# A decoder layer on one core: weight buffers 4160 and 4128 bytes apart instead of 4096

## The chip, the cores and the metric

The kernel runs on one NeuronCore of a Trainium2 chip. The metric is device time in microseconds. The kernel before takes 413.82 us, the median of three runs (413.51, 413.82, 414.05). Work is spread over TensorE (PE; its weight loads are listed as PEld), VectorE (DVE), ScalarE (ACT), GpSimd (POOL) and SyncE (SP, which issues the loads of weights). SBUF is the on-chip memory of 128 partitions; a tile takes the same range of bytes in each partition, and that range's start is called its place here.

## The reference

One hybrid decoder layer in float32 on 256 tokens with D = 1024. Two token mixers (an RWKV-7 recurrence and causal attention over one block of 256) read one combined projection; their outputs are gated, merged and projected; a gated MLP with a width-3 causal convolution follows.

```
h = rms_norm(x, norm1_g);  proj = h @ w_in              # 1024 x 5408
y_a = rwkv7_time_mix(shifted part of proj)              # 8 heads of 64
y_b = moba_attention(q, k, v)                           # 8 heads of 64
x = x + (sigmoid(g_a) * (y_a @ w_branch_a) + sigmoid(g_b) * (y_b @ w_branch_b)) @ w_out
h2 = rms_norm(x, norm2_g);  u = h2 @ w_ffn_up           # 1024 x 5632
x = x + (gelu(causal_conv3(u[:, :2816])) * u[:, 2816:]) @ w_ffn_down
```

## The kernel before

Every big product is split for precision. A weight tile of 128 x 1024 float32 (4 KB in a partition) is loaded into a `raw` buffer. ScalarE rounds it to TensorE's shorter format into a `whi` buffer (line 238, in a few early cases VectorE), and VectorE writes the remainder raw - whi into a `wlo` buffer (line 248). Activations are split in the same way (`hh` and `hl` are the two halves of `hx`; `mh`/`ml`, `yah`/`yal`, `ybh`/`ybl` and `hb` are others). A product is then the sum of three: high x high, high weight x low activation, low weight x high activation.

Four `raw`, four `whi` and three `wlo` buffers rotate (line 51). `weights` hands out a ready pair and makes the next; `load_next` issues the next load on SP. Each matmul has one operand that is loaded into the array (128 columns) and one that is streamed past it (256 or 512 columns). Which is which differs:

- `wst` (lines 278, 280, 283): weights loaded, 256 columns of activations streamed. Most projections and both branch products.
- `xst` (lines 299, 300, 303): activations loaded, 512 columns of weights streamed. The attention's projections (with `hx`) and the output projection (with `mh`, `ml`).
- `up` (lines 1160, 1163), the FFN's first product: weights loaded, `hx` streamed, 512 columns for the high weights (both halves of the activations at once) and 256 for the low ones.
- `down` (lines 1178, 1180, 1182), its second: `hb` loaded, 512 columns of weights streamed.

The pools of tiles lie one behind the other in a partition: `cst` (constants, `hx`, and the four buffers that hold `yah`, `yal`, `ybh`, `ybl` among others), then `wp` (`raw`, `whi`, `wlo`), then `sb` (everything else: x, `hb`, `mh`, `ml`, the work tiles). Places in bytes, as the program is built:

| tile | before | modulo 512 |
|---|---|---|
| hx (cst) | 29760 | 64 |
| ybh, ybl, yah, yal (cst) | 46144, 50240, 54336, 58432 | 64 |
| raw, four | 71040 and every 4096 | 384 |
| whi, four | 87424 and every 4096 | 384 |
| wlo, three | 103808 and every 4096 | 384 |
| first tile of sb | 116096 | 384 |
| hb, eight places | 124288 to 161152 | 384 |
| ml, mh | 165248, 189824 | 384 |

Of the kernel before, what the change touches and what calls it, by code (L numbers as in the profile page):

```python
# [9 lines left out]
F32 = mybir.dt.float32  # L10
F32R = mybir.dt.float32r
# [25 lines left out]
def body(tc, x, positions, norm1_g, w_in, rwkv_mu, w_decay_up, decay_bias, w_aaa_up,  # L37
# [5 lines left out]
    with ctx:  # L43
        cst = ctx.enter_context(tc.tile_pool(name="cst", bufs=1))
        wp = ctx.enter_context(tc.tile_pool(name="wp", bufs=1))
        sb = ctx.enter_context(tc.tile_pool(name="sb", bufs=1))
        ps = ctx.enter_context(tc.tile_pool(name="ps", bufs=1, space=PSUM))
        dr = ctx.enter_context(tc.tile_pool(name="dr", bufs=1, space=DRAM))

        joined = [False]  # L50
        NB4, NRAW, NHI, NLO = 10, 4, 4, 3

# [166 lines left out]
        def load_next(first=False, into=None):  # L219
            if queue:  # L220
                ap = queue.pop(0)
                k, c = ap.shape[1], ap.shape[2]
                raw = wp.tile([128, 1024], F32, name="raw", tag="raw", bufs=NRAW) if into is None else into
                rv = raw[:, :k * c].rearrange("p (k c) -> p k c", k=k)
                for ks in ((slice(0, 2), slice(2, 4)) if first else (slice(0, k),)):
                    nc.sync.dma_start(rv[:, ks], ap[:, ks])
                raws.append((raw, k, c))
# [3 lines left out]
        def split_hi():  # L231
            if raws:
                nhi[0] += 1
                eng = dve if nhi[0] in (4, 5, 6) else act
                raw, k, c = raws.pop(0)
                hi = wp.tile([128, 1024], F32R, name="whi", tag="whi", bufs=NHI)
                if eng is act:
                    act.copy(hi[:, :k * c], raw[:, :k * c])  # L238
                else:
                    eng.tensor_copy(hi[:, :k * c], raw[:, :k * c])  # L240
                halves.append((raw, hi, k, c))

        def split_lo(eng=dve):
            if halves:
                raw, hi, k, c = halves.pop(0)
                n = k * c
                lo = wp.tile([128, 1024], F32R, name="wlo", tag="wlo", bufs=NLO)
                eng.tensor_tensor(lo[:, :n], raw[:, :n], hi[:, :n].bitcast(F32), op=OP.subtract)  # L248
                ready.append((hi[:, :n].rearrange("p (k c) -> p k c", k=k),
                              lo[:, :n].rearrange("p (k c) -> p k c", k=k)))  # L250
                nlo[0] += 1
                if not NRAW < nlo[0] <= NRAW + 4:
                    load_next()

        def weights(n=1):

            w = ready.pop(0)
            for _ in range(n):
                split_lo()
                split_hi()  # L260
            return w
# [76 lines left out]
        def first_steps():  # L338
# [58 lines left out]
                                         hh[:, k].bitcast(F32), op0=OP.mult, op1=OP.subtract)  # L397

            def tiles(nm):
                return wp.tile([128, 1024], F32R, name=nm, tag=nm, bufs=NHI if nm == "whi" else NLO)  # L400


            raw, _, _ = raws.pop(0)
            hi, lo = tiles("whi"), tiles("wlo")
            hs = [slice(i * 512, i * 512 + 512) for i in range(2)]
            dve.tensor_copy(hi[:, hs[0]], raw[:, hs[0]])
# [7 lines left out]
            for k in range(4):  # L414
                low(k)
            split_hi()
            high(6)
            high(7)
            for k in range(4, 8):
                low(k)  # L420
            split_lo()
            split_hi()
            split_lo()
            split_hi()
            p = acc()
# [846 lines left out]
```

## Time and profile before

| | before |
|---|---|
| median of the timed runs, us | 413.82 |
| the profiled execution, us | its span, 411.9; the page has no other time of it |
| HBM read, written | 68.76 MB, 1.44 MB, 170 GB/s over the span |
| TensorE busy from 210 to 306 us (the FFN) | 96.00 of 96.00 us |
| VectorE busy in that stretch | 76.52 us |
| ScalarE busy in that stretch | 55.42 us |
| costliest lines of the chain | acc L1160 15%, acc L1163 7%, L278, L280 and L283 7% each |

A row of the groups reads: line, engine, operation, output<-inputs, shapes, xcount, then the busy time in us and the mean duration of one in ns, then the idle time of the engine just ahead and what ended it. Matmul records overlap each other, since the engine is pipelined. A row with three durations gives the shortest, the median and the longest.

### The profile page before, as it was taken

The page shows a single profiled execution, that of the slowest core. Times are in us where ns is not written, and L with a number is a line of the kernel's source. Part 1 is how long each engine was busy: PE and PEld are TensorE (multiplying, and loading weights), DVE is VectorE, ACT ScalarE, POOL GpSimd, SP SyncE. Part 2 cuts the span into 40 slices and gives each one's busy share as a digit, 9 for nine tenths or more (in the row PEclk, how much of TensorE's full clock was granted, in tenths as well). Part 3 has the DMA queues.
Part 4 walks back from the last instruction along what each step waited for, and adds up shares of the span by engine and source line. Part 5 has one row for each costly group of instructions (what it writes and reads, how often), then busy time and mean ns, then how long its engine had stood idle before and what let it go on. Part 6 is the DMA issues. An engine that isn't in the chain of part 4 may idle for free.

```text
span 411.9 us, 8111 instructions
## 1 busy us (share of the span) xinstructions
PE 404.6 (98%) x3199; PEld 355.6 (86%) x3199; DVE 322.2 (78%) x559; ACT 230.8 (56%) x384; POOL 38.3 (9%) x62
## 2 busy tenths in 40 slices
PE   6999999999999999999999999999999999999996
PEld 3999989888899998999988888888888888888885
DVE  2888999869557876678974898979779678797784
ACT  5799645465444765453653884646446455464450
POOL 8910070000210010120000000000000000000000
PEclk9999999999999999999999999999999999999999
DMA  8955565663483352466564555765665666656612
GB/s 247 314 190 154 156 179 157 163 171 105 95 226 94 104 155 68 146 202 198 175 197 147 160 199 183 225 202 176 199 193 171 199 200 198 200 168 199 198 53 102
DMA packets 61765, 70.72 MB, mean 172 GB/s; under 512 B 8349, under 2 KB 52195, under 8 KB 61728
## 3 DMA queue, kind: packets, MB, share of 16 engines
q1 hardware_dynamic: 60768, 69.41, 56.3%
q0 software_dynamic: 944, 0.80, 0.9%
q8 instruction: 25, 0.41, 0.4%
q14 instruction: 12, 0.10, 0.1%
q10 hardware_dynamic: 16, 0.00, 0.0%
HBM read 68.76 MB, written 1.44 MB: 170 GB/s over the span
## 4 chain that ended last, share of the span: by engine, by line
PE 89%; DVE 4%; ACT 3%; DMA 1%; issue 1%; SPq 0%; POOL 0%; ACTq 0%
PE acc L1160 15%; PE acc L1163 7%; PE acc L278 7%; PE acc L283 7%; PE acc L280 7%; PE at L1160 5%; PE acc L299 5%; PE f L1182 4%; PE acc L303 4%; PE f L1180 4%; PE acc L300 4%; PE f L1178 4%; PE at L1163 2%; ACT sc L970 2%; DMA x<-in_x_dram 1%
## 5 line engine op out<-in xcount | busy, mean ns | idle before, releaser
L238 ACT CAST whi<-raw 128x1024 fp32r<-128x1024 f32 x120 | 125.8, 1051 | 113.6 <-PE acc L1160 26.2
L248 DVE TENSOR_TENSOR wlo<-raw,whi 128x1024 fp32r<-128x1024 f32 x120 | 145.7, 1218 | 41.8 <-PE acc L1163 12.9
L1160 PE MATMUL acc<-hx,whi 128*128 128x512 f32 x264 | 72.4, 395 | 0.0
L278 PE MATMUL acc<-hx,whi 128*128 128x256 f32 x232 | 58.2, 287 | 0.0
L280 PE MATMUL acc<-hx,whi 128*128 128x256 f32 x232 | 56.0, 278 | 0.0
L1160 PEld LDWEIGHTS acc<-hx,whi 128*128 128x128 f32 x264 | 45.3, 188 | 6.3
L1163 PEld LDWEIGHTS acc<-hx,wlo 128*128 128x128 f32 x264 | 40.2, 188 | 6.1
L278 PEld LDWEIGHTS acc<-hx,whi 128*128 128x128 f32 x232 | 43.6, 188 | 1.6 <-issue 0.7
L280 PEld LDWEIGHTS acc<-hx,whi 128*128 128x128 f32 x232 | 43.7, 188 | 0.1
L1163 PE MATMUL acc<-hx,wlo 128*128 128x256 f32 x264 | 41.3, 278 | 0.0
L283 PE MATMUL acc<-hx,wlo 128*128 128x256 f32 x232 | 35.9, 277 | 0.0
L1182 PE MATMUL f<-wlo,hb 128*128 128x512 f32 x80 | 31.3, 391 | 0.0
L1180 PE MATMUL f<-whi,hb 128*128 128x512 f32 x80 | 31.2, 390 | 0.0
L1178 PE MATMUL f<-whi,hb 128*128 128x512 f32 x80 | 31.2, 390 | 0.0
L283 PEld LDWEIGHTS acc<-hx,wlo 128*128 128x128 f32 x232 | 30.7, 188 | 0.3 <-issue 0.3
L1160 PE MATMUL at<-hx,whi 128*128 128x512 f32 x88 | 24.0, 394 | 0.0
L1168 DVE TENSOR_REDUCE an<-acc 128x256 f32<-128x512 f32 x22 | 15.0, 689 | 6.5 <-PE acc L1163 5.6
L299 PE MATMUL acc<-whi,hx 128*128 128x512 f32 x48 | 19.3, 403 | 0.0
L300 PE MATMUL acc<-whi,hx 128*128 128x512 f32 x48 | 18.8, 391 | 0.0
L1182 PEld LDWEIGHTS f<-wlo,hb 128*128 128x128 f32 x80 | 15.0, 188 | 3.5 <-DVE wlo L248 0.4
L1178 PEld LDWEIGHTS f<-whi,hb 128*128 128x128 f32 x80 | 15.0, 188 | 2.8
L1180 PEld LDWEIGHTS f<-whi,hb 128*128 128x128 f32 x80 | 15.0, 188 | 2.8
(311 smaller groups left out, 700.4 us busy)
## 6 DMA issues: line engine op xcount, KB each, us to landing
raw<-in_w_ffn_up_dram SPq DMA_DIRECT2D x44, 512.0 KB, 4.3
raw<-in_w_in_dram SPq DMA_DIRECT2D x38, 512.0 KB, 4.5
raw<-in_w_ffn_down_dram SPq DMA_DIRECT2D x22, 512.0 KB, 3.3
raw<-in_w_out_dram SPq DMA_DIRECT2D x8, 512.0 KB, 4.3
x<-in_x_dram SPq DMA_DIRECT2D x8, 256.0 KB, 5.2
early<-in_w_in_dram SPq DMA_DIRECT2D x4, 512.0 KB, 9.8
raw<-in_w_branch_b_dram SPq DMA_DIRECT2D x4, 512.0 KB, 3.6
raw<-in_w_branch_a_dram SPq DMA_DIRECT2D x4, 512.0 KB, 4.1
```

Source lines behind the costliest of these rows:

```text
L238: act.copy(hi[:, :k * c], raw[:, :k * c])
L248: eng.tensor_tensor(lo[:, :n], raw[:, :n], hi[:, :n].bitcast(F32), op=OP.subtract)
L278: pe.matmul(om, wh[:, k, ms], xh[:, k0 + k], start=k0 + k + m == 0, stop=False, skip_group_check=True)
L280: pe.matmul(om, wh[:, k, ms], xl[:, k0 + k], start=False, stop=False, skip_group_check=True)
L283: pe.matmul(om, wl[:, k, ms], xh[:, k0 + k], start=False, stop=k0 + k == nk - 1 and m == n - 1, skip_group_check=True)
L299: pe.matmul(ps_[t], xh[:, K, ts], wh[:, k], start=K == 0, stop=False)
L300: pe.matmul(ps_[t], xl[:, K, ts], wh[:, k], start=False, stop=False)
L1160: pe.matmul(ps_[m], wh[:, k, ms], hx[:, k0 + k].rearrange("p a s -> p (a s)"), start=k0 + k == 0, stop=False, skip_group_check=True)
L1163: pe.matmul(ps_[m][:, 0:S], wl[:, k, ms], hh[:, k0 + k], start=False, stop=k0 + k == 7, skip_group_check=True)
L1178: pe.matmul(fin[f], hb[:, 0, i, ts], wh[:, 0, cs], start=st, stop=False, skip_group_check=f == 3)
L1180: pe.matmul(fin[f], hb[:, 1, i, ts], wh[:, 0, cs], start=False, stop=False, skip_group_check=f == 3)
L1182: pe.matmul(fin[f], hb[:, 0, i, ts], wl[:, 0, cs], start=False, stop=False, skip_group_check=f == 3)
```

## The change

The `whi` tiles are made 1040 elements wide in place of 1024 (4160 bytes), the `wlo` tiles 1032 (4128 bytes); the first 1024 of them are used, as before. At the start of `sb` a tile of 40 elements that nobody uses is added.

```diff
+        sb.tile([128, 40], F32, name="gap")
         joined = [False]
...
-                hi = wp.tile([128, 1024], F32R, name="whi", tag="whi", bufs=NHI)
+                hi = wp.tile([128, 1040], F32R, name="whi", tag="whi", bufs=NHI)
...
-                lo = wp.tile([128, 1024], F32R, name="wlo", tag="wlo", bufs=NLO)
+                lo = wp.tile([128, 1032], F32R, name="wlo", tag="wlo", bufs=NLO)
...
             def tiles(nm):
-                return wp.tile([128, 1024], F32R, name=nm, tag=nm, bufs=NHI if nm == "whi" else NLO)
+                return wp.tile([128, 1040 if nm == "whi" else 1032], F32R, name=nm, tag=nm,
+                               bufs=NHI if nm == "whi" else NLO)[:, 0:1024]
```

Every instruction stands where it stood on each of the five engines, with the same shapes; their operands' places differ:

| tile | after | moved by | modulo 512 |
|---|---|---|---|
| hx, ybh, ybl, yah, yal, raw | as before | 0 | as before |
| whi, four | 87424, 91584, 95744, 99904 | 0, 64, 128, 192 | 384, 448, 0, 64 |
| wlo, three | 104064, 108192, 112320 | 256, 288, 320 | 128, 160, 192 |
| all of sb | 512 further (4 x 64 + 3 x 32 + 160) | 512 | as before |

## The prediction

> **What bounds the kernel now.** I read the page first (busy shares, the chain that ended last), then the groups of instructions with shapes kept apart, then the same groups cut to short windows, because the change moves no instruction and only a group whose members differ for no visible reason can be reached by it.
>
> ```profile
> span 411.9 us, 8111 instructions
> PE 404.6 (98%) x3199; PEld 355.6 (86%) x3199; DVE 322.2 (78%) x559; ACT 230.8 (56%) x384; POOL 38.3 (9%) x62
> PEclk9999999999999999999999999999999999999999
> PE 89%; DVE 4%; ACT 3%; DMA 1%; issue 1%; SPq 0%; POOL 0%; ACTq 0%
> L238 ACT CAST whi<-raw 128x1024 fp32r<-128x1024 f32 x120 | 125.8, 1051 | 113.6 <-PE acc L1160 26.2
> L248 DVE TENSOR_TENSOR wlo<-raw,whi 128x1024 fp32r<-128x1024 f32 x120 | 145.7, 1218 | 41.8 <-PE acc L1163 12.9
> ```
>
> The chain is TensorE for 89% of the span, at the full granted clock. The two instructions that write the changed buffers, ScalarE's cast and VectorE's subtraction, stood idle for 113.6 and 41.8 us ahead of these groups, mostly until TensorE had released something. So the matmuls decide, and the others run in their shadow.
>
> A matmul's record is longer than its share of the engine. In the FFN's down product:
>
> ```profile
> 300.05 0.39 PE L1178 MATMUL f<-whi,hb 128*128 128x512 f32 x1
> 300.27 0.39 PE L1180 MATMUL f<-whi,hb 128*128 128x512 f32 x1
> 300.50 0.39 PE L1182 MATMUL f<-wlo,hb 128*128 128x512 f32 x1
> 300.73 0.39 PE L1178 MATMUL f<-whi,hb 128*128 128x512 f32 x1
> ```
>
> Three starts take 300.73 - 300.05 = 0.68 us, 227 ns each, while a record is 0.39 us. Records overlap by a fixed 0.16 us, so a *difference* of two mean durations is a difference of time on the engine. With that, equal matmuls are compared:
>
> ```profile
> L1160 PE MATMUL acc<-hx,whi 128*128 128x512 f32 x264 | 72.4, 395 | 0.0
> L1160 PE MATMUL at<-hx,whi 128*128 128x512 f32 x88 | 24.0, 394 | 0.0
> L1163 PE MATMUL acc<-hx,wlo 128*128 128x256 f32 x264 | 41.3, 278 | 0.0
> L1163 PE MATMUL at<-hx,wlo 128*128 128x256 f32 x88 | 13.7, 277 | 0.0
> L1182 PE MATMUL f<-wlo,hb 128*128 128x512 f32 x80 | 31.3, 391 | 0.0
> L1178 PE MATMUL f<-whi,hb 128*128 128x512 f32 x80 | 31.2, 390 | 0.0
> ...
> L303 PE MATMUL acc<-wlo,hx 128*128 128x512 f32 x48 | 14.9, 393 | 0.0
> L303 PE MATMUL acc<-wlo,mh 128*128 128x512 f32 x32 | 9.9, 390 | 0.0
> ...
> L299 PE MATMUL acc<-whi,hx 128*128 128x512 f32 x11 | 4.3, 393 | 0.0
> L300 PE MATMUL acc<-whi,hx 128*128 128x512 f32 x11 | 4.3, 391 | 0.0
> L303 PE MATMUL acc<-wlo,hx 128*128 128x512 f32 x10 | 3.1, 390 | 0.0
> ...
> L299 PE MATMUL acc<-whi,mh 128*128 128x512 f32 x6 | 2.3, 389 | 0.0
> L300 PE MATMUL acc<-whi,ml 128*128 128x512 f32 x6 | 2.3, 389 | 0.0
> L303 PE MATMUL acc<-wlo,mh 128*128 128x512 f32 x6 | 1.8, 389 | 0.0
> ...
> L278 PE MATMUL acc<-hx,whi 128*128 128x256 f32 x36 | 8.7, 276 | 0.0
> ...
> L278 PE MATMUL acc<-hx,whi 128*128 128x256 f32 x15 | 3.7, 281 | 0.0
> ...
> L278 PE MATMUL acc<-yah,whi 128*128 128x256 f32 x32 | 7.9, 281 | 0.0
> L280 PE MATMUL acc<-yal,whi 128*128 128x256 f32 x31 | 7.7, 281 | 0.0
> L283 PE MATMUL acc<-yah,wlo 128*128 128x256 f32 x28 | 4.4, 281 | 0.0
> ```
>
> The first eight rows are of the whole program (the L303 ones give the counts, which L299 and L300 share; L1180 counts as L1178; waits are in their means); then come windows at 50 to 57, 201.5 to 205.5, 24 to 36, 63.5 to 68 and 187 to 201 us. Two things are to be seen. L299 to L303 are the same code in both windows, yet take 389 ns throughout with mh and ml as the loaded operand and 390 to 393 with hx. And L278 runs at 276 ns for one whole stretch and at 281 for others, with the same operands. So TensorE has a fast and a slow pace, and something of operand and history picks it.
>
> The operands' places in the partition fit. Before the change raw, whi, wlo, hb, mh and ml all begin at 384 modulo 512 bytes, while hx and the branches' yah, yal, ybh, ybl begin at 64. Call d the loaded operand's place less the streamed one's, modulo 512. The pairs with d = 0 (down, and mh/ml) sit at 389 to 391; hx under whi (d = 192) at 390 to 393; whi under hx (d = 320) at 394 to 395, or in the narrow ones at 276 or 281. That is a reading of few rows, and place could stand for something else (below).
>
> **The change part by part.** No instruction is added, removed or moved: on each of the five engines the order is the same row for row. No semaphore and no buffer count changes, so no wait is added. What is left are places: the four whi buffers move by 0, 64, 128 and 192 bytes, the three wlo buffers by 256, 288 and 320, and all tiles behind them by 512, which is nothing modulo 512.
>
> *What the slow pace costs now*, the most there is to gain, with 389 and 276 as the fast durations:
> - FFN up, wide: 264 x 6 + 88 x 5 ns = 2.02 us.
> - FFN up, narrow: 264 x 2 + 88 x 1 = 0.62 us.
> - Projections and branches at 281: the rows above hold 15 + 32 + 31 + 28 = 106 such matmuls; with L280 and L283 of the window from 63.5 (14 and 12) and the ybh and ybl rows of the window from 187 (30), quoted next, 162 x 5 = 0.81 us.
> - Projections at 512 columns: (4 + 2 + 1) ns per three, 48 threes, 0.34 us.
>
> ```profile
> L280 PE MATMUL acc<-hx,whi 128*128 128x256 f32 x14 | 3.5, 281 | 0.0
> L283 PE MATMUL acc<-hx,wlo 128*128 128x256 f32 x12 | 1.9, 281 | 0.0
> ...
> L278 PE MATMUL acc<-ybh,whi 128*128 128x256 f32 x9 | 2.3, 281 | 0.0
> L280 PE MATMUL acc<-ybl,whi 128*128 128x256 f32 x9 | 2.3, 281 | 0.0
> L283 PE MATMUL acc<-ybh,wlo 128*128 128x256 f32 x12 | 1.9, 281 | 0.0
> ```
>
> Together 3.8 us, 0.9% of the span. If every place mattered and all became good, that is the gain.
>
> *What the new places do to it.* The trace shows three values of d; a price for the others is an estimate of mine from those rows: 0 ns at d = 0, 2.3 at 192 (the mean of 4, 2 and 1), 5.7 at 320 (2.02 us over 352 wide matmuls), straight lines between and back to 0 at 512. Per wide matmul this gives 1.9 at 448, 3.8 at 384, 4.0 at 256, 3.2 at 224 and 0.8, 1.2, 1.5 at 64, 96, 128.
> - FFN up, wide: d was 320 and becomes 320, 384, 448, 0 with the buffer; mean 2.85, so 352 x 2.85 = 1.0 us less.
> - FFN up, narrow: d becomes 64, 96, 128, mean 1.2 against 5.7, a fifth; 0.5 us less.
> - The narrow projections and branches: two matmuls in three load whi (half the price), one wlo (a fifth); 0.6 of 0.81 = 0.5 us less.
> - 512-column projections: d becomes 192, 128, 64, 0 for whi (1.35 mean; 96 x 0.95 = 0.09 us less), 448, 416, 384 for wlo (2.9; 48 x 0.6 = 0.03 more).
> - Down and the output projection lose what they have. Their d was 0; for whi it becomes 0, 448, 384, 320: mean 2.85 on 160 + 64 matmuls, 0.64 us more. For wlo 256, 224, 192: mean 3.2 on 80 + 32, 0.35 us more.
>
> Sum: -1.0 - 0.5 - 0.5 - 0.1 + 1.0 = **-1.1 us**.
>
> *The other engines.* VectorE's subtraction reads raw and whi and writes wlo; the first two now lie apart.
>
> ```profile
> L248 DVE TENSOR_TENSOR wlo<-raw,whi 128x1024 fp32r<-128x1024 f32 x120 | 145.7, 1218 | 41.8 <-PE acc L1163 12.9 <-PE acc L303 8.8 <-ACT whi L238 6.5
> L1217 DVE TENSOR_TENSOR cv<-cv,bs 128x256 f32<-128x256 f32 x22 | 9.0, 419 | 0.0
> ```
>
> (1218 - 419) / 768 = 1.04 ns an element, the same step from tiles of 1 KB to tiles of 4 KB; nothing in it looks like two reads in each other's way. I take 0 for it and for the cast. If the cast got 18 ns slower or faster (an estimate: a quarter of the 73 between its shortest and longest below), 120 of them are 2 us of an engine that idles for longer beside TensorE: nothing on the path, and 2 us if that cover were gone.
>
> ```profile
> L238 ACT CAST whi<-raw x120: 1029/1052/1102, 12.0 to 397.1; 128x1024 fp32r<-128x1024 f32 x120
> ```
>
> *The second wlo buffer* starts 32 bytes off a multiple of 64, as no streamed weight does now. L303 and L1182 stream wlo 160 times, a third from that buffer: 53 matmuls. I take 0; between a gain and a loss of the slow pace's 6 ns each it is 0.3 us either way.
>
> A rule speaks against the change. The Trainium skill, "SBUF — State Buffer", section "Who interferes with whom", gives TensorE two independent read ports, for the streamed operand and the loaded one, says that it never waits on anyone, and names a port that VectorE and GpSimd share as the only point of contention on the engines' side. By that the bytes between buffers are worth nothing, and 413.8 would stay. The 389 against 393 ns of one and the same line is more than that rule accounts for, but no run here has moved a buffer yet.
>
> **Rivals.**
> - *Places don't matter; only history does.* The pace is set by the phase in which a stretch of matmuls begins. For: one line at one d runs at 276 or 281. Against: with mh/ml and in down, the pace settles at 389. Also, what I call place could be region: hx lies low in the partition beside whi, hb and mh far above. Then nothing changes: 413.8, with 413.5 to 414.1 as the runs before spread.
> - *The good pairs are spoiled and the bad ones stay bad* (slower). The mechanism: d = 0 alone is safe, and any other d lets a load fall into the stream. Place: down (240 matmuls) and the output projection (96), which hold the fast pace now. Price: 6 ns each, 336 x 6 = 2.0 us; then less the quarter of FFN up's whi loads that come to d = 0, 0.5 us. That is 415.3; each further 100 narrow matmuls that fall to 281 add 0.5 us. It decides against me once more than half of down's matmuls leave 389 while L1160 stays above 393.
> - *The rotation breaks the slow pace everywhere.* With d changing at every tile no slow phase is kept: -3.8 us, 410.0.
>
> **How the numbers follow.** The profiled execution's span is 411.9 us and the page has no other time of it; the median of the timed runs, 413.82, is 1.9 above, taken as the launch and the end around the span, unchanged. My sum gives 413.82 - 1.1 = **412.7 us**, faster by 0.26%; 0.2%, or 0.8 us, is about what a measurement can tell from none. This mechanism I hold at 0.43, with sums from -0.3 to -2.2 us (a fifth of that chance falls inside 0.2%); nothing at all 0.29; spoiled pairs 0.20 (nearly all over 0.2% slower); broken everywhere 0.08. Faster: 0.35 + 0.08 = 0.43; same: 0.08 + 0.29 = 0.37 less 0.01 that drifts slower = 0.36; slower 0.21. The range leaves out about half of the last rival below and half of the spoiled case above: 410.6 to 415.3 us.
>
> **What would show it.** Right: L1160's mean falls from 395 towards 392, with members at 389 where the fourth whi buffer is loaded; L1163 goes to 276; L1178 to L1182 rise by 2 to 4 ns. Wrong on places: L1160's repeating pattern and L299's 393 against 389 stay as they are. Wrong in sign: L1178 to L1182 near 396. Wrong on the cover: L238 or L248 with another mean duration and TensorE's busy share under 98%.

## The result, and the profile after

The changed kernel took 417.73 us, the median of four runs (416.94 to 418.46), against 413.76 of the kernel before beside it: a ratio of 1.0089, with a 95% interval from 1.0071 to 1.0106. It is slower by 4.0 us between the medians, or 0.9% by the ratio. The prediction was 412.7 us in a range from 410.6 to 415.3.

First the page of the changed kernel, with the lines that answer to those of before (line numbers are up to two higher, in some of the runs further down up to four; L239 is the cast, L249 the subtraction).

```profile
span 416.2 us, 8111 instructions
PE 408.9 (98%) x3199; PEld 358.4 (86%) x3199; DVE 322.4 (77%) x559; ACT 230.7 (55%) x384; POOL 37.6 (9%) x62
PE 89%; DVE 4%; DMA 2%; ACT 2%; issue 1%; SPq 0%; ACTq 0%
L239 ACT CAST whi<-raw 128x1024 fp32r<-128x1024 f32 x120 | 125.5, 1050 | 116.8 <-PE acc L1162 30.9
L249 DVE TENSOR_TENSOR wlo<-raw,whi 128x1024 fp32r<-128x1024 f32 x120 | 145.8, 1219 | 43.5 <-PE acc L1165 13.0
```

The span is 4.3 us longer, and TensorE's busy time is 4.3 us longer (404.6 to 408.9). The cast and the subtraction take what they took (1051 and 1218 before), although whi and wlo moved. So the time went into the matmuls themselves, not into a wait. The groups with shapes kept apart say which; columns are shapes, count, busy us, mean ns of one:

```profile
L1162 PE MATMUL acc<-hx,whi 128*128 128x512 f32 x264 | 72.3, 395 | 0.0
L279 PE MATMUL acc<-hx,whi 128*128 128x256 f32 x232 | 59.2, 289 | 0.0
L281 PE MATMUL acc<-hx,whi 128*128 128x256 f32 x232 | 57.0, 280 | 0.0
L1165 PE MATMUL acc<-hx,wlo 128*128 128x256 f32 x264 | 42.1, 281 | 0.0
L284 PE MATMUL acc<-hx,wlo 128*128 128x256 f32 x232 | 36.6, 280 | 0.0
L1184 PE MATMUL f<-wlo,hb 128*128 128x512 f32 x80 | 31.5, 394 | 0.2 <-DVE wlo L249 0.2
L1182 PE MATMUL f<-whi,hb 128*128 128x512 f32 x80 | 31.4, 393 | 0.0
L301 PE MATMUL acc<-whi,hx 128*128 128x512 f32 x48 | 18.9, 394 | 0.0
L1165 PE MATMUL at<-hx,wlo 128*128 128x256 f32 x88 | 13.9, 280 | 0.0
L301 PE MATMUL acc<-whi,ml 128*128 128x512 f32 x32 | 12.6, 393 | 0.0
```

The same groups of the kernel before that the prediction didn't show:

```profile
L278 PE MATMUL acc<-hx,whi 128*128 128x256 f32 x232 | 58.2, 287 | 0.0
L280 PE MATMUL acc<-hx,whi 128*128 128x256 f32 x232 | 56.0, 278 | 0.0
L283 PE MATMUL acc<-hx,wlo 128*128 128x256 f32 x232 | 35.9, 277 | 0.0
L1180 PE MATMUL f<-whi,hb 128*128 128x512 f32 x80 | 31.2, 390 | 0.0
L300 PE MATMUL acc<-whi,hx 128*128 128x512 f32 x48 | 18.8, 391 | 0.0
L300 PE MATMUL acc<-whi,ml 128*128 128x512 f32 x32 | 12.5, 389 | 0.0
```

Differences of means times counts: the narrow projections 232 x (2 + 2 + 3) ns = 1.6 us; up's narrow ones 264 x 3 + 88 x 3 = 1.1; down 240 x 3 = 0.7; the output projection 96 x 4 = 0.4; the 512-column projections about 0.2; up's wide ones 0. Together 4.0 of the 4.3 us. This loss is spread over more than a thousand matmuls, some 3 ns each, and no chain or wait names it.

### The profile page after: what moved, and what is told of

Same layout as the page of the kernel before. It is cut to its first block, busy times and chain, and to the rows that moved or that the text cites. A ratio compares the mean times of both kernels' runs of the same rounds, so it can differ in the third digit from the quotient of the medians.

```text
span 416.2 us, 8111 instructions
## 1 busy us (share of the span) xinstructions
PE 408.9 (98%) x3199; PEld 358.4 (86%) x3199; DVE 322.4 (77%) x559; ACT 230.7 (55%) x384; POOL 37.6 (9%) x62
## 4 chain that ended last, share of the span: by engine, by line
PE 89%; DVE 4%; DMA 2%; ACT 2%; issue 1%; SPq 0%; ACTq 0%
PE acc L1162 12%; PE acc L279 9%; PE acc L284 8%; PE acc L281 8%; PE acc L1165 6%; PE acc L300 5%; PE acc L304 4%; PE acc L301 4%; PE f L1184 4%; PE f L1182 4%; PE f L1180 4%; PE at L1162 4%; PE at L1165 2%; DVE wlo L249 2%; DMA x<-in_x_dram 1%; DMA raw<-in_w_ffn_up_dram 1%
## 5 line engine op out<-in xcount | busy, mean ns | idle before, releaser
L239 ACT CAST whi<-raw 128x1024 fp32r<-128x1024 f32 x120 | 125.5, 1050 | 116.8 <-PE acc L1162 30.9
L249 DVE TENSOR_TENSOR wlo<-raw,whi 128x1024 fp32r<-128x1024 f32 x120 | 145.8, 1219 | 43.5 <-PE acc L1165 13.0
L1162 PE MATMUL acc<-hx,whi 128*128 128x512 f32 x264 | 72.3, 395 | 0.0
L279 PE MATMUL acc<-hx,whi 128*128 128x256 f32 x232 | 59.2, 289 | 0.0
L281 PE MATMUL acc<-hx,whi 128*128 128x256 f32 x232 | 57.0, 280 | 0.0
L1162 PEld LDWEIGHTS acc<-hx,whi 128*128 128x128 f32 x264 | 45.6, 188 | 6.6
L1165 PEld LDWEIGHTS acc<-hx,wlo 128*128 128x128 f32 x264 | 40.5, 188 | 5.8
L281 PEld LDWEIGHTS acc<-hx,whi 128*128 128x128 f32 x232 | 43.8, 189 | 0.1
L1165 PE MATMUL acc<-hx,wlo 128*128 128x256 f32 x264 | 42.1, 281 | 0.0
L284 PE MATMUL acc<-hx,wlo 128*128 128x256 f32 x232 | 36.6, 280 | 0.0
L1184 PE MATMUL f<-wlo,hb 128*128 128x512 f32 x80 | 31.5, 394 | 0.2 <-DVE wlo L249 0.2
L284 PEld LDWEIGHTS acc<-hx,wlo 128*128 128x128 f32 x232 | 31.3, 188 | 0.3 <-issue 0.3
L1182 PE MATMUL f<-whi,hb 128*128 128x512 f32 x80 | 31.4, 393 | 0.0
L1162 PE MATMUL at<-hx,whi 128*128 128x512 f32 x88 | 24.0, 394 | 0.0
L300 PE MATMUL acc<-whi,hx 128*128 128x512 f32 x48 | 19.3, 403 | 0.0
L1184 PEld LDWEIGHTS f<-wlo,hb 128*128 128x128 f32 x80 | 15.0, 188 | 4.1 <-DVE wlo L249 0.7
L1182 PEld LDWEIGHTS f<-whi,hb 128*128 128x128 f32 x80 | 15.0, 188 | 3.0
```

The source lines that it names most:

```text
L279: pe.matmul(om, wh[:, k, ms], xh[:, k0 + k], start=k0 + k + m == 0, stop=False, skip_group_check=True)
L281: pe.matmul(om, wh[:, k, ms], xl[:, k0 + k], start=False, stop=False, skip_group_check=True)
L284: pe.matmul(om, wl[:, k, ms], xh[:, k0 + k], start=False, stop=k0 + k == nk - 1 and m == n - 1, skip_group_check=True)
L300: pe.matmul(ps_[t], xh[:, K, ts], wh[:, k], start=K == 0, stop=False)
L1162: pe.matmul(ps_[m], wh[:, k, ms], hx[:, k0 + k].rearrange("p a s -> p (a s)"), start=k0 + k == 0, stop=False, skip_group_check=True)
L1165: pe.matmul(ps_[m][:, 0:S], wl[:, k, ms], hh[:, k0 + k], start=False, stop=k0 + k == 7, skip_group_check=True)
```

## The experiments

Three theories stood after the result. **Difference**: the loaded operand's place less the streamed one's decides. **Line**: an operand's own place decides, multiples of 128 bytes being good. **Rotation**: only a change of place from tile to tile costs. All kernels compute the whole layer. Spare tiles keep everything else where it was modulo 512. The first four runs moved hx and the branch buffers, to 384 and to 128 modulo 512, and staggered whi alone, by 128 and by 64 bytes.

hx and the branch buffers at 384, so that all operands begin at the same place:

```diff
+        cst.tile([128, 80], F32, name="padhx")
         hx = cst.tile([128, 8, 2, S], F32R, name="hx", tag="hx")
...
             L = by("L")
+            cst.tile([128, 48], F32, name="padkb")
```

> The weights stay 4096 bytes apart; hx and the four branch buffers move by 320 bytes, so that every operand of the big products begins at 384 modulo 512. Difference theory (loaded place less streamed place, modulo 512, decides; 0 is free): the wide up matmuls fall from 395 to 389 and no stretch runs at 281; about 410, 3.8 us faster. Line theory (an operand that does not begin at a multiple of 128 bytes costs; hx is the one of before): the same, about 410. Rotation theory (only a change of place from tile to tile costs): 413.8, as before, since every tile of a kind has one place.

417.42 us against 414.1, ratio 1.0083 (1.0056 to 1.011). Groups as above:

```profile
L1162 PE MATMUL acc<-hx,whi 128*128 128x512 f32 x264 | 72.2, 394 | 0.0
L280 PE MATMUL acc<-hx,whi 128*128 128x256 f32 x232 | 58.0, 283 | 0.0
L1165 PE MATMUL acc<-hx,wlo 128*128 128x256 f32 x264 | 42.3, 281 | 0.0
L300 PE MATMUL acc<-whi,hx 128*128 128x512 f32 x48 | 18.7, 390 | 0.0
```

This miss was the most useful of all. No tile rotates through places here, so rotation isn't needed for a loss, and every operand is a multiple of 128 bytes, so the line theory falls too. The difference 0, which the prediction took as free, is *slow* for the narrow matmuls (283 against 278) and good for the 512-column ones that load hx (390 against 391). Each shape has its own price.

hx at 128 modulo 512 (pads of 16 and 112 elements in place of 80 and 48):

> As the run with hx at 384, but hx and the branch buffers begin at 128 modulo 512: a multiple of 128 bytes, but 256 away from the weights. Difference theory: no better than before, 413 to 415, wide up matmuls at 393 or more. Line theory: about 410, as with hx at 384. Rotation theory: 413.8.

417.86 against 414.1, ratio 1.0097 (1.0067 to 1.0127), with the rows of the run before it within 1 ns (two of them):

```profile
L280 PE MATMUL acc<-hx,whi 128*128 128x256 f32 x232 | 58.0, 283 | 0.0
L300 PE MATMUL acc<-whi,hx 128*128 128x512 f32 x48 | 18.7, 391 | 0.0
```

Places 256 bytes apart are alike: the period is 256 bytes or a part of it, not the 512 that the prediction assumed.

whi 128 bytes further apart, and whi alone as in the change (`tiles`, which makes the first pair, gets the same widths in both):

```diff
-                hi = wp.tile([128, 1024], F32R, name="whi", tag="whi", bufs=NHI)
+                hi = wp.tile([128, 1056], F32R, name="whi", tag="whi", bufs=NHI)
```

> The whi buffers 4224 bytes apart (128 more), the wlo buffers 4096 apart at their old place modulo 512. Rotation theory: two thirds of the weights that are loaded or streamed change place from tile to tile, so about two thirds of the loss comes back: 416 to 417. Line theory: every place is a multiple of 128 as before, 413.8. Difference theory: differences of 320, 448, 64, 192 in the up products and 0, 384, 256, 128 in down; 414 to 416.

414.56 against 414.1, ratio 1.0019 (1.0004 to 1.0034).

```diff
-                hi = wp.tile([128, 1024], F32R, name="whi", tag="whi", bufs=NHI)
+                hi = wp.tile([128, 1040], F32R, name="whi", tag="whi", bufs=NHI)
...
-            hi, lo = tiles("whi"), tiles("wlo")
+            hi = tiles("whi")
+            wp.tile([128, 64], F32, name="padlo")
+            lo = tiles("wlo")
```

> The change's whi buffers alone (4160 apart); wlo 4096 apart at its old place modulo 512. Line theory: two of four whi buffers are off a multiple of 128; about half to two thirds of the loss, 415.5 to 416.5. Rotation theory: 416 to 417, as with 128 bytes. If the loss hangs on wlo alone (its 32-byte steps, or its being 256 away from whi): 413.8.

416.91 against 414.1, ratio 1.0076 (1.0048 to 1.0103). First the groups of the stagger by 128, then those of the stagger by 64:

```profile
L280 PE MATMUL acc<-hx,whi 128*128 128x256 f32 x232 | 56.6, 279 | 0.0
L1181 PE MATMUL f<-whi,hb 128*128 128x512 f32 x80 | 31.3, 391 | 0.0
```

```profile
L280 PE MATMUL acc<-hx,whi 128*128 128x256 f32 x232 | 57.2, 280 | 0.0
L1166 PE MATMUL acc<-hx,wlo 128*128 128x256 f32 x264 | 41.9, 280 | 0.0
L1183 PE MATMUL f<-whi,hb 128*128 128x512 f32 x80 | 31.5, 394 | 0.0
```

Three of four tiles change place in both, yet only one costs much, so rotation as such is not the price. The wlo row of the second run rose from 278 to 280 although wlo stayed: a slow pace carries over to neighbours. In the change, in this run and in the one below on wlo alone the projections' wlo matmuls all took 280 ns (277 before), whichever of the two moved.

The second four mapped the differences between, and split the change's other half off. hx at 96 and at 32 modulo 128 (pads of 8 and 24 elements):

> Weights 4096 apart as before; hx and the branch buffers at 96 modulo 128, so that the loaded weight lies 32 ahead of the streamed activation modulo 128 (before: 64; with hx at 128 or 384: 0). Theory of the difference modulo 128, each shape with its own best: narrow matmuls of the projections between 278 (64) and 283 (0), so L280 near 280 to 281, L1163 near 280, and 415 to 416.5. If 64 is no optimum but one point on a slope, one of this run and its twin at 32 is under 413. Theory that any place that is a multiple of 64 is alike and only 0 is bad: 413.8.

417.03 against 413.73, ratio 1.0084 (1.0063 to 1.0105).

> As the run before it, with hx and the branch buffers at 32 modulo 128 (difference 96). Difference modulo 128: L280 280 to 281, 415 to 416.5; if a slope runs through 64, one of the two runs is under 413.

416.79 against 413.73, ratio 1.0074 (1.0057 to 1.0091). Both times are a little over the expected 415 to 416.5, and neither run is faster than before. Groups of hx at 96, then of hx at 32:

```profile
L280 PE MATMUL acc<-hx,whi 128*128 128x256 f32 x232 | 57.4, 281 | 0.0
L300 PE MATMUL acc<-whi,hx 128*128 128x512 f32 x48 | 19.0, 395 | 0.0
L1180 PE MATMUL f<-whi,hb 128*128 128x512 f32 x80 | 31.2, 390 | 0.0
```

```profile
L280 PE MATMUL acc<-hx,whi 128*128 128x256 f32 x232 | 56.9, 279 | 0.0
L300 PE MATMUL acc<-whi,hx 128*128 128x512 f32 x48 | 19.0, 395 | 0.0
```

Down, whose operands did not move, stays at 390 in the first: what changes there is only what touches hx. Not all of that changes: up's wide matmuls (L1162, output in `acc`) took 394 to 396 wherever hx was put, against 395 before.

The change's wlo alone (1032 elements, a pad of 64 ahead of the first, 40 at the start of the tiles behind):

> The change's wlo buffers alone (4128 apart, 256 further on), whi 4096 apart at its old place. Difference modulo 128: of the three wlo buffers one keeps 64 against hx, one comes to 96, one to 0; L1163 rises from 278 to about 280, L283 from 277 to 279 or 280, L280 stays at 278; 414.8 to 415.6, and with the run on whi alone (2.8 us) the two parts add up to the change's 3.7 to 4.0. If whi alone holds the loss: 413.8.

416.17 against 413.73, ratio 1.0064 (1.0045 to 1.0082); more than expected.

```profile
L281 PE MATMUL acc<-hx,whi 128*128 128x256 f32 x232 | 56.1, 278 | 0.0
L1167 PE MATMUL acc<-hx,wlo 128*128 128x256 f32 x264 | 41.9, 280 | 0.0
L1184 PE MATMUL f<-whi,hb 128*128 128x512 f32 x80 | 31.5, 394 | 0.0
L1186 PE MATMUL f<-wlo,hb 128*128 128x512 f32 x80 | 31.8, 397 | 0.0
```

L281 and L1167 do as foretold. What I had not foretold is down: L1184 streams whi, which did not move, and rose from 390 to 394, in step with the wlo matmuls between. The two halves are 2.8 and 2.4 us and the whole is 4.0: they overlap, since each spoils matmuls of the other's.

Only the tiles behind the weights moved, by 64 bytes:

```diff
+        sb.tile([128, 16], F32, name="gap")
         joined = [False]
```

> Only the tiles behind the weights move, by 64 bytes: hb, mh and ml come to 64 modulo 128, against the weights' 0. Difference modulo 128: down and the output projection, at 389 to 391 before, behave like the projections that load hx at 64: L1178 to L1182 at 392 to 393; all else unchanged; 414.3 to 414.8. If the weights' own places decide: 413.8.

415.72 against 413.73, ratio 1.0054 (1.0036 to 1.0071).

```profile
L281 PE MATMUL acc<-hx,whi 128*128 128x256 f32 x232 | 56.0, 278 | 0.0
L1183 PE MATMUL f<-wlo,hb 128*128 128x512 f32 x80 | 31.7, 397 | 0.2 <-DVE wlo L249 0.2
L1181 PE MATMUL f<-whi,hb 128*128 128x512 f32 x80 | 31.6, 395 | 0.0
L301 PE MATMUL acc<-whi,ml 128*128 128x512 f32 x32 | 12.6, 394 | 0.0
```

The weights and hx are where they were, the projections run as before, and down and the output projection lose 4 to 6 ns each. The tiles that VectorE and ScalarE work in moved as well, yet up, beside which they work, stayed at 395 and 278 (L1161, L1164): what slowed are the matmuls that read a moved tile, not those beside moved work of other engines. But hx under whi, also 64 away modulo 128, had taken only 391. Either the period is 256 (192 there, 64 here) or hx differs from hb in some other way. The last of the mapping runs ask that.

hx at 192 modulo 512 (pads of 32 and 96), hx at 0 (112 and 16), and everything from hx on moved by 64 with all differences kept (one pad of 16):

> hx and the branch buffers at 192 modulo 512, weights 4096 apart at 384. Loaded less streamed: 192 modulo 256 in the projections and up (64 before), 64 in the 512-column projections that load hx (192 before). Difference modulo 128: nothing changes, 413.8. Difference modulo 256: L300 goes from 391 to 394 or 395, what L1181 and L301 took at 64 in the run with the tiles behind the weights moved; L280 is open between 276 and 283, about 414 to 417.

415.68 against 414.06, ratio 1.0034 (1.002 to 1.0047).

> hx and the branch buffers at 0 modulo 512: loaded less streamed is 384, that is 0 modulo 128 and 128 modulo 256. Difference modulo 128: as with hx at 384 and at 128, L280 at 283, L300 at 390, 417 to 418. Difference modulo 256: L280 leaves 283 and L300 leaves 390; if 128 is a place that neither load nor stream disturbs, under 413.

418.3 against 414.06, ratio 1.0098 (1.0079 to 1.0117).

> Everything from hx on moves by 64 bytes; every difference is as before, every place is another one. Difference theory, modulo whatever: L280 at 278, L300 at 391, L1180 at 390, 413.8. Theory of the place itself (multiples of 128 are good or bad by themselves): hx now is one and the weights, hb, mh and ml are none; a loss of 2 us or more.

413.9 against 414.06, ratio 0.9992 (0.9978 to 1.0005). Groups of the three runs in this order:

```profile
L280 PE MATMUL acc<-hx,whi 128*128 128x256 f32 x232 | 57.1, 279 | 0.0
L300 PE MATMUL acc<-whi,hx 128*128 128x512 f32 x48 | 19.0, 397 | 0.0
L1162 PE MATMUL at<-hx,whi 128*128 128x512 f32 x88 | 23.7, 391 | 0.0
```

```profile
L280 PE MATMUL acc<-hx,whi 128*128 128x256 f32 x232 | 57.6, 282 | 0.0
L300 PE MATMUL acc<-whi,hx 128*128 128x512 f32 x48 | 18.9, 394 | 0.0
```

```profile
L280 PE MATMUL acc<-hx,whi 128*128 128x256 f32 x232 | 55.9, 277 | 0.0
L300 PE MATMUL acc<-whi,hx 128*128 128x512 f32 x48 | 18.8, 391 | 0.0
L1181 PE MATMUL f<-whi,hb 128*128 128x512 f32 x80 | 31.2, 390 | 0.0
```

With a period of 128 the first of these would have left L300 at 391, and the second would have left it at 390. They went to 397 and 394, so the period is 256. And where everything from hx on moves by these 64 bytes and no difference does, rows and time stay: nothing is left for the place itself.

The mean durations by difference (loaded less streamed, modulo 256), from the rows above and of before, where all matmuls of a group had one difference:

| difference | narrow, whi loaded, L280 | 512 columns of weights streamed |
|---|---|---|
| 0 | 283, 283 | 390, 391 with hx; 390 with hb |
| 32 | 281 | 395 |
| 64 | 278 (before) | 397 with hx; 394 to 397 with hb and ml |
| 128 | 282 | 394 |
| 192 | 279 | 391 (before) |
| 224 | 279 | 395 |

96 and 160 were not tried for whole groups. These are means of groups, and what a matmul takes depends on its neighbours too: in the run on wlo alone the differences in L1186 are among 0, 192 and 224, none over 395 in the table, and it took 397.

The run with hx at 192 suggests one gain: up's wide matmuls took 391 there with the output in `at` (394 before). So the last run put hx of the FFN alone there (the first hx keeps elements 0 to 4096 of the wider tile):

```diff
-        hx = cst.tile([128, 8, 2, S], F32R, name="hx", tag="hx")
+        hx = cst.tile([128, 4224], F32R, name="hx", tag="hx")[:, 32:4128]
+        hx = hx.rearrange("p (k a s) -> p k a s", k=8, a=2)
```

> The weights as before; the hx of the FFN alone begins 128 bytes further on (192 modulo 512), the first hx and the branch buffers stay at 64. Difference modulo 256, priced by the runs so far: up goes to the difference 192, where the run with hx at 192 had L1162 at 394 and 391 and L1165 at 278 and 279; projections, branches, down and the output projection keep theirs. 0.4 us faster than before, 413.4 to 413.7. If the differences of the three stages did not act apart from each other: as with all of hx at 192, 415 to 416.

413.5 against 413.88, ratio 0.9997 (0.9986 to 1.0008).

```profile
L1162 PE MATMUL acc<-hx,whi 128*128 128x512 f32 x264 | 72.1, 394 | 0.0
L1162 PE MATMUL at<-hx,whi 128*128 128x512 f32 x88 | 23.7, 391 | 0.0
L1165 PE MATMUL acc<-hx,wlo 128*128 128x256 f32 x264 | 41.3, 278 | 0.0
L1165 PE MATMUL at<-hx,wlo 128*128 128x256 f32 x88 | 13.9, 279 | 0.0
```

The rows do what was foretold (264 x 1 + 88 x 3 - 88 x 2 ns = 0.35 us less), and the stages act apart from each other here: of the other large groups none rose by more than 1 ns. In time it is a tie: no version tried is measurably faster than the kernel before.

## Why the prediction was wrong

**What bounds the kernel** was right. TensorE carries 89% of the chain before and after, the lost time is all in its matmuls, and the other engines' two instructions cost the same within 1 ns.

**That the difference of places acts on the pace** was right, and the rival that places mean nothing, with region in its stead, fell: 64 bytes on the tiles behind the weights (hb, mh and ml among them) cost 2.0 us, and 64 bytes on everything from hx on cost nothing. The rival's other half, that history picks the pace, holds in part (below). The Trainium skill, "SBUF — State Buffer", section "Who interferes with whom", by which TensorE's two read ports are independent and it never waits on anyone, would have left 413.8. The measurement decides against that here: moving hx alone among the operands of L280 took it from 278 to 283 ns. What in the memory or in TensorE does it, these runs do not show.

**The step that failed** is "a price for the others ... 0 ns at d = 0 ... straight lines between", one curve for every shape and a period of 512. The 0 was read from 512-column matmuls and carried over to the narrow ones. There it is the worst place measured: 283 against 278. The kernel before sat at 64, the best of the six tried for the narrow matmuls (by 1 ns), with 0 for down and the output projection, the best tried for 512 columns of weights. Every stagger that was tried left them in part.

**A second reading failed with it**, under the largest gain: "5.7 at 320 (2.02 us over 352 wide matmuls)" takes the 394 to 395 ns of up's wide matmuls for the price of their difference. With hx at 384 that difference was 0, the place called free, and L1162 still took 394; over all the places of hx its means are 394 to 396 in `acc` and 391 to 395 in `at`. So there was little to win by a change of place. Why these matmuls run at 394 stays open.

With the table the means of the change can be worked out. The whi differences are 64, 128, 192 and 0 in the narrow projections: (278 + 282 + 279 + 283) / 4 = 280.5, and L281 took 280. In down they are 0, 192, 128 and 64: (390 + 391 + 394 + 397) / 4 = 393, and L1182 took 393. Only the first holds in its parts. The weight tiles take the four whi buffers in turn, so the trace can be taken apart by buffer: L281 then has 278, 282, 278 and 281 ns, within 2 ns of the table, but L1182 has 394, 394, 393 and 390, lowest where the table has 397. The same weight tile, whose whi has the difference 64 in both, in the change (window 284.26 to 287.20 us) and in the run that staggers whi alone by 64 (284.45 to 287.45):

```profile
L1182 PE MATMUL f<-whi,hb 128*128 128x512 f32 x4 | 1.6, 390 | 0.0
L1183 PE MATMUL f<-whi,hb 128*128 128x512 f32 x4 | 1.6, 397 | 0.0
```

whi and hb lie alike, modulo 512, in these two; only the places of wlo, which the neighbouring matmuls stream, differ. In down a matmul's pace is therefore not a price of its own two places, and that the mean came out at 393 is luck.

**Term by term.** FFN up, wide: -1.0 foretold, 0 measured (the second reading above). Up, narrow: -0.5 foretold, +1.1 measured. The narrow projections (with the branches): -0.5 foretold, +1.6 measured in the projections. Down and the output projection: +1.0 foretold, 0.7 + 0.4 = 1.1 measured; the only term with the right size, though by buffer the prices under it were not those that ran (390 ns at 64, 394 at 0). The 512-column projections: -0.1 foretold, +0.2 measured (the mean of the four whi prices there is 1.15 ns, not the 1.35 of the prediction, which moves the sum by 0.02 us).

**The slower rival** had the right place for that part and half its price right (3 to 4 ns each, not 6). The sign it named came: most of down's matmuls left 389 while L1162 stayed at 395. But it saw 2.0 us of loss in down and the output projection, and the narrow runs at 281 as a small addition; these were 2.7 of the 4.0 us.

**The range** failed with the price curve: its upper end came from that rival, with no case in which the narrow matmuls all lose. The trace held a warning: they ran at 276 and at 281 at the same difference, so their fast pace was the one that could be lost.

## What to carry to other kernels

When a run is bound by back-to-back matmuls, the places of the loaded and the streamed operand relative to each other can matter: here they were worth up to 1%, and no wait and no chain showed it, only the mean durations of equal matmuls; compare these across stages and between versions whenever a tile's size changes. A best place for one shape can be the worst for another, so a price read from one group should not be carried to the next without a run, and a mean that fits is no proof of its parts. Here tiles of a whole 4096 bytes, which all begin at one place, were better than any stagger that was tried.

## What the runs showed of the hardware that was not expected

The difference of the two operands' places acts modulo 256 bytes: hx 256 bytes further gave the same rows within 1 ns, 128 further did not (L300 391 and 397). The narrow matmuls' means (L280) lie between 277 and 283 ns and those that stream 512 columns of weights (L300, L1178 to L1182) between 389 and 397, and a slow pace carries to neighbours whose own operands did not move: L1184 of the run on wlo alone took 394, 390 before. The reverse is there too: one weight tile's four matmuls at one difference took 390 in the change and 397 with wlo elsewhere. What keeps whole stretches of the kernel before at 281 and others at 276 at one difference stays open.
